# A two-layer hybrid block on one core: S5's backward rows in reverse order of time, and recurrent gates by 64-feature blocks, issued in steps

## The chip, the core and the metric

The kernel runs on one core of one Trainium2 chip. The metric is the device time of one execution in microseconds. An engine's name stands for its hardware: PE is TensorE, DVE VectorE, ACT ScalarE, POOL GpSimd, SP SyncE, whose queue issues the DMAs.

## The reference

Two layers act on 1024 latent and 256 context tokens of 1024 features. Cut to what matters here, a layer is

```python
h = _rmsnorm(x, norm_g[l]) * (1.0 + scale[:, None]) + shift[:, None]
ckv, krope, u_s5, x_lru, cq, x_pool, gpath, mlogit = jnp.split(h @ w_in[l], IN_SPLITS, axis=-1)
...
r = jax.nn.sigmoid(_block_diag(x, w_a, b_a).astype(f32))      # RG-LRU, both directions
i = jax.nn.sigmoid(_block_diag(x, w_x, b_x).astype(f32))      # 4 blocks of 64 x 64
log_a = -LRU_C * r * jax.nn.softplus(-lam.astype(f32))
b = jnp.sqrt(-jnp.expm1(2.0 * log_a)) * (i * x.astype(f32))
...
hc_re, hc_im = _s5_states(ucg, zero, zero, disc, rev)         # S5, dr = 0 and 1
hl_re, hl_im = _s5_states(ug, hc_re[:, last], hc_im[:, last], disc, rev)
y = y + _s5_readout(hl_re, hl_im, c_re[dr], c_im[dr])
...
y = y + jax.nn.sigmoid(ml[n]) * ((branches[n] * jax.nn.silu(gp[n])) @ w_branch[n])
```

Four branches read one projection `h @ w_in` of 6304 columns: latent attention (MLA), a diagonal state-space model of 16 groups with 64 states in either direction of time (S5), a gated linear recurrence in both directions (RG-LRU), and pooling. Each branch is multiplied by its gate path and projected, the four are summed under merge gates, `y @ w_out` follows, and the residual. The second layer needs no context output.

## The kernel before

**Tiles and products.** Features lie on partitions, tokens along the free side in three chunks `CH`: 256 context tokens and twice 512 latent ones. h, the normalised input of the layer, stays in SBUF as two float32r parts, high and low. A projection tile of 128 features and one chunk (`hgemm`, L181) is eight K-tiles of three float32r passes each (`gemm`, L174: low weight on high h, high on low, high on high), summed in a PSUM bank `pg`. `load_w` (L158) brings 128 x 512 weights by SyncE into a raw tile `wr` (two buffers); ScalarE copies the high part `wh`, VectorE subtracts for the low part `wl`. For the small weights of the branches these are `wph` and `wpl`. PSUM holds two banks `pg`, three `pS`, two `pm` and one `pP`. All matmuls go through the helper at L135, all ScalarE activations through L132, two-operand VectorE work through L117 and L120, and DMAs through L111, so operations are told apart by the tiles' names.

**The order.** The tile scheduler puts instructions in order by priority, which follows the text of the program except where a `with self.hp()` block lifts it. A tile that reuses memory waits for the last reader of what was there. Pools open by phase: `pr` and `pa` for the first part of a layer, `p5` with `pt` (attention) and then `pc` (merge) inside it, `pd` for the output projection. A layer (L1124) runs in this order: latent projections and keys (`mla_in`, `mla_kv`), the S5 input (`s5_in`), the recurrence's input and convolution (`lru_in`), `lru`, the query latents (`cq_in`), queries (`mla_q`), the pooling input (`pool_in`), pooling between gate tiles, attention, the other gate tiles, merge logits of the pooling branch, the merge, and the output projection.

**RG-LRU** (`lru`, L584). The weights of all gates, `wg`, come in one load as 128 x 128 matrices with two 64 x 64 blocks on the diagonal and zeros beside them. For each half f of the features, direction d and chunk, two float32 products with the tile `xl` give both gates, in a bank `pm` and a bank `pS`; one Tanh each takes 128 partitions out of it, to `l1` and `l2`. After the three chunks come Exp, Tanh, Square and Sqrt on ScalarE, products and scans over all tokens on VectorE, and after both directions a DMA of the branch output to DRAM.

**S5** (`s5`, L820) works on eight groups of two per layer. It is a Python generator: `logits` and `merge` step it between their tiles, and `lead` says how many steps lie between its parts. In a group the tokens are folded eight to a column: 160 columns, and `SC` = 192 with the 32 context columns once more behind the latent ones. The 128 partitions are 64 states forward and 64 backward. VectorE builds weights (`er`, `wb`, `wc`, `wk`) and phases (`ph`, from `hun`), both by way of `tm`; TensorE forms the inputs in `pS`, ScalarE copies them to `rqx`, VectorE rotates them by `ph`, scans them with a real decay, forward rows from column 0 up and backward rows from column 191 down, and rotates back into `er`; TensorE reads `er` with `wc` into `pS` (`pS<-er,wc`).

**Merge** (`merge`, L1020) goes over pooling, RG-LRU, MLA and S5 in that order. For each branch it multiplies output and gate (two loads `og`, then `b`), and for each of eight feature tiles j it makes the merge logits (not for pooling, whose logits were made before), the branch product `pm<-b,wph` / `wpl`, and the sum into `y`. `out_proj` (L1089) reads `ox`, the old x, by DMA, and forms the new one. Both `og` and `ox` are tiles of one tag in the standing pool `stream`, two buffers.

Of the kernel before, what the change touches and what calls it, by code (L numbers as in the profile page):

```python
# [42 lines left out]
V_D, V_CW, V_CB, V_LAM, V_BA, V_BX, V_PB, V_PS = 39, 41, 49, 51, 55, 59, 63, 65  # L43
NV = 67
# [19 lines left out]
class Net:  # L64
# [93 lines left out]
    def load_w(self, src, nk, small=False):  # L158
# [3 lines left out]
        with self.hp():  # L162
            for i in range(0, nk * m, 512):
# [3 lines left out]
                hi = self.whl.tile([128, w], F32R, tag=th, name=self.name(th), **kw)  # L167
                lo = self.whl.tile([128, w], F32R, tag=tl, name=self.name(tl), **kw)
# [19 lines left out]
    def prologue(self):  # L188
# [20 lines left out]
        self.ones, self.halfpi, self.halves, self.sgn = k[:, 0:1], k[:, 1:2], k[:, 2:4], k[:, 4:5]  # L209
# [220 lines left out]
    def cq_in(self, l, m, lat, pa):  # L430
# [153 lines left out]
    def lru(self, l, xls, oD, outs, pa, pr):  # L584
        nc, I, vec = self.nc, self.I, self.vec[l]
# [3 lines left out]
        hba = sp[:, 24:32]  # L589
# [15 lines left out]
        self.ts(hba, vec[:, V_BA:V_BA + 8], 0.5, None, ALU.mult, None)  # L605
        wg = self.t(pa, "wg", 1024)
        self.dma(wg, I["w_lru"][l])
        wgv = view(wg, 2, 2, 2, 128)
        for f in range(2):
            xl = xls[f]  # L610
            y = self.t(pr, "ly", NT)
            for d in range(2):
                c = 2 * d + f
                col = lambda a: a[:, c:c + 1]
                tr, ti, a, th = (self.t(pr, n_, w_)[:, 0:NT] for n_, w_ in (("l1", 1312), ("l2", 1312), ("l3", 8 * SC), ("l4", 8 * SC)))
                for s0, n in CH:
                    for g, dst in ((0, tr), (1, ti)):
                        ps = (self.pS() if g else self.ps())[:, 0:n]
                        self.mm(ps, wgv[:, d, g, f], xl[:, s0:s0 + n])
                        self.act(dst[:, s0:s0 + n], ps, AF.Tanh, bias=hba[:, 4 * g + c:4 * g + c + 1], scale=0.5)  # L620
# [16 lines left out]
            o0 = CH[outs[0]][0]  # L637
            self.dma(oD[f][:, o0:], y[:, o0:])


    def pool_in(self, l, lat, pa):
# [91 lines left out]
    def s5_head(self, l, p5):  # L733
# [86 lines left out]
    def s5(self, l, uF, uD, oD, lat, p5, lead):  # L820

# [15 lines left out]
        for q in range(16 // G):  # L837
# [595 lines left out]
```

## Time and profile before

| | |
|---|---|
| median of 3 runs | 2319.51 us (2313.85, 2319.51, 2320.29) |
| the profiled execution | 2318.8 us |
| its span on the core | 2317.0 us |
| mean granted TensorE clock | 0.996 |
| busy: TensorE, VectorE, ScalarE, GpSimd | 2265.9, 1545.9, 963.1, 208.7 us |
| mean busy share of the 16 DMA engines | 32.2% by the hardware queue |

The span is the time from the first to the last instruction of the profiled execution; its own time is 1.8 us longer. A busy time is the union of an engine's instructions. Matmuls are pipelined and overlap, so a record's duration is longer than what the pass costs; what it costs is the distance from its start to the next one's start. A granted clock of 1.00 is 2.4 GHz, a clock of 0.5 is 1.2 GHz, and a mean between them says that both were granted in the stretch. "Idle before" is the idle time of an engine just before a group of instructions, with what ended it.

### The profile page before, as it was taken

Reading aid. Unit: us, or ns where it says so; the run is one execution under the profiler, and the core shown is the slowest. Engines: PE = TensorE matmul, PEld = TensorE weight load, DVE = VectorE, ACT = ScalarE, POOL = GpSimd, SP = SyncE. Lnnn points to the kernel's source line nnn. Section 1 sums busy time; section 2 is a strip of 40 time slices with the busy share of each in tenths; the row PEclk is TensorE's granted clock in tenths of the full one; section 3 lists DMA queues with packets and bytes.
Section 4 is the critical chain, followed back from the end, with each engine's and each line's share of the span. In section 5 each row is a group of like instructions: output and inputs, shape, how many; then the busy total and the mean of one; then the engine's idle time right before and its main releaser. Section 6 shows DMA issues by size and latency. Waiting matters only on the chain.

```text
span 2317.0 us, 33029 instructions
## 1 busy us (share of the span) xinstructions
PE 2265.9 (98%) x11680; PEld 1847.4 (80%) x11680; DVE 1545.9 (67%) x3528; ACT 963.1 (42%) x1954; POOL 208.7 (9%) x261
## 2 busy tenths in 40 slices
PE   8999999999999999999999999999999899999999
PEld 3787878888788888788888787788888788877887
DVE  5665669776877888656455746688667878863253
ACT  4546656665312222312143436756664232322131
POOL 0000000000001121111122100000000011211100
PEclk9999999999999999999999999999999999999999
DMA  8150332211533223423334331332214331232134
GB/s 279 59 162 35 112 118 69 72 57 54 175 97 120 74 77 107 131 90 106 98 100 155 122 122 65 112 117 72 72 55 127 109 108 50 85 112 86 46 117 156
DMA packets 215750, 236.34 MB, mean 102 GB/s; under 512 B 78112, under 2 KB 141344, under 8 KB 215584
## 3 DMA queue, kind: packets, MB, share of 16 engines
q1 hardware_dynamic: 215072, 234.19, 32.2%
q8 instruction: 92, 1.51, 0.3%
q0 software_dynamic: 512, 0.03, 0.1%
q14 instruction: 74, 0.61, 0.1%
HBM read 175.70 MB, written 58.46 MB: 101 GB/s over the span
## 4 chain that ended last, share of the span: by engine, by line
PE 49%; DVE 5%; DMA 2%; ACT 1%; issue 1%; POOL 0%; SPq 0%; ACTq 0%; DVEq 0%; POOLq 0%
PE pg L135 34%; PE pS L135 6%; PE pm L135 5%; PE pP L135 3%; PE pm L138 1%; DVE wl L117 1%; DVE tm L117 1%; DVE st L120 1%; DMA wr<-in_w_out 1%; DMA s5g<-y 1%; DMA wr<-in_w_in 0%; DVE h L120 0%; PE pS L138 0%; ACT pt L132 0%; DVE er L117 0%
## 5 line engine op out<-in xcount | busy, mean ns | idle before, releaser
L135 PE MATMUL pg<-h,wh 128*128 128x512 f32 (+1 forms) x4608 | 1346.2, 374 | 0.2 <-DVE h L117 0.2
L135 PEld LDWEIGHTS pg<-h,wh 128*128 128x128 f32 x4608 | 829.0, 189 | 153.7 <-issue 4.5
L135 PE MATMUL pg<-h,wl 128*128 128x512 f32 (+1 forms) x2304 | 871.1, 378 | 1.8 <-DVE wl L117 1.6
L135 PEld LDWEIGHTS pg<-h,wl 128*128 128x128 f32 x2304 | 434.4, 189 | 80.5 <-issue 3.6
L117 DVE TENSOR_TENSOR wl<-wr,wh 128x512 fp32r<-128x512 f32 x268 | 190.5, 713 | 167.0 <-ACT wh L132 165.7
L132 ACT ACTIVATE wh<-wr 128x512 fp32r<-128x512 f32 x268 | 167.9, 628 | 272.9 <-PE pg L135 148.3
L132 ACT ACTIVATE st<-pg 128x512 f32<-128x512 f32 (+1 forms) x200 | 110.4, 552 | 350.9 <-PE pg L135 339.7
L117 POOL TENSOR_TENSOR y<-y,st 128x512 f32<-128x512 f32 (+1 forms) x120 | 153.6, 1280 | 733.8 <-DVE st L120 703.6
L135 PE MATMUL pm<-b,wph 128*128 128x512 f32 (+1 forms) x640 | 184.6, 373 | 1.6 <-DVE b L117 1.6
L132 ACT ACTIVATE P<-pS,sm,qs 128x512 f32<-128x512 f32 (+1 forms) x200 | 138.6, 702 | 45.3 <-DVE sm L124 43.2
L120 DVE SCALAR_TENSOR_TENSOR st<-st,pm 128x512 f32<-128x512 f32 (+1 forms) x120 | 75.6, 630 | 105.8 <-PE pm L135 105.3
L135 PE MATMUL pS<-k,q 128*128 128x512 f32 (+1 forms) x600 | 145.2, 365 | 0.5 <-DVE q L117 0.3
L135 PEld LDWEIGHTS pm<-b,wph 128*128 128x128 f32 x640 | 115.9, 189 | 24.4 <-DVE b L117 3.1
L135 PE MATMUL pP<-pt,v 128*128 128x256 f32 x656 | 126.9, 301 | 3.5 <-DVE pt L117 1.3
L135 PEld LDWEIGHTS pP<-pt,v 128*128 128x128 f32 x656 | 99.0, 188 | 35.6 <-ACT pt L132 21.9
L135 PE MATMUL pm<-b,wpl 128*128 128x256 f32 (+1 forms) x320 | 120.1, 376 | 5.0 <-ACT b L132 2.8
L117 DVE TENSOR_TENSOR pt<-pm,pt 128x512 fp32r<-128x512 f32 x164 | 106.9, 683 | 26.2 <-ACT pt L132 25.4
L518 DVE TENSOR_REDUCE sm<-pS 128x1 f32<-128x512 f32 (+1 forms) x200 | 113.3, 586 | 15.0 <-PE pS L135 13.1
L132 ACT ACTIVATE pt<-pm 128x512 fp32r<-128x512 f32 x164 | 91.0, 599 | 70.6 <-PE pm L138 70.1
L135 PEld LDWEIGHTS pS<-k,q 128*128 128x128 f32 x600 | 98.8, 189 | 18.0 <-ACT P L132 4.5
L138 PE MATMUL pm<-ident,P 128*128 128x128 f32 x656 | 106.3, 274 | 0.2 <-ACT P L132 0.2
L120 DVE SCALAR_TENSOR_TENSOR pP<-wa,cv,pP 128x256 f32<-128x256 f32 x196 | 95.3, 486 | 14.1 <-DMA wa<-in_w_ada 10.4
(244 smaller groups left out, 2500.2 us busy)
## 6 DMA issues: line engine op xcount, KB each, us to landing
wr<-in_w_in SPq DMA_DIRECT2D x196, 256.0 KB, 2.7
wa<-in_w_ada SPq DMA_DIRECT2D x96, 256.0 KB, 2.9
wr<-in_w_out SPq DMA_DIRECT2D x64, 256.0 KB, 2.9
gD<-st SPq DMA_DIRECT2D x32, 256.0 KB, 2.0
tD<-st SPq DMA_DIRECT2D x32, 256.0 KB, 2.2
og<-oD SPq DMA_DIRECT2D x32, 256.0 KB, 2.7
og<-gD SPq DMA_DIRECT2D x32, 256.0 KB, 2.9
wr<-in_w_branch SPq DMA_DIRECT2D x64, 128.0 KB, 2.0
```

The costliest lines, as they stand in the source:

```text
L117: (eng or self.nc.vector).tensor_tensor(out=out, in0=a, in1=b, op=op)
L120: self.nc.vector.scalar_tensor_tensor(out=out, in0=a, scalar=s, in1=b, op0=op0, op1=op1)
L132: self.nc.scalar.activation(out=out, in_=a, func=func, scale=scale, **kw)
L135: self.nc.tensor.matmul(out=out, lhsT=lhsT, rhs=rhs, start=start, stop=stop)
L138: self.nc.tensor.transpose(out=out, in_=in_, identity=ident)
L518: nc.vector.tensor_reduce(out=mx3[:, i:i + 1], in_=S, axis=AX.X, op=ALU.max)
```

## The change

**S5.** The backward rows are copied out of PSUM in reverse order of time, from columns 32 to 191, so that both directions run over 160 columns from the first to the last; the copy to `rqx` becomes two, of 64 partitions each. Phases, rotation and scan have 160 columns a group in place of 192, the two scans of 64 partitions become one of 128, and the read-back turns the backward rows round again.

**The recurrence's gates.** `xb` holds two stacked versions of `xl`, one per block b of 64 features: its own 64 rows carry the high float32r part, the other 64 the low part. The weights come per direction and half, 128 x 256, by the raw tiles `wr`, stacked to fit: `wgh` is the high part of the block's two gate matrices in both halves of the rows, `wgl` the low part on the block's own rows and zero on the others (GpSimd's memset). A gate tile is then two accumulated float32r passes for each block, `wgl` and `wgh`, and comes out of PSUM in two Tanh of 64 partitions, one per gate.

**The steps.** `lru` becomes a generator that stops after the first latent chunk of each (f, d) and after each (f, d). `cq_in` and `pool_in` step it after each latent chunk, eight times in all, and `pool_in` moves ahead of `mla_q`. The output DMA goes out after d = 1 of each half.

**Pools.** `og` and `ox` move from `stream` to `pc` and `pd`, `wph` and `wpl` from the standing weight pool to `pc`.

```diff
-                hi = self.whl.tile([128, w], F32R, tag=th, name=self.name(th), **kw)
-                lo = self.whl.tile([128, w], F32R, tag=tl, name=self.name(tl), **kw)
+                pool = small or self.whl
+                hi = pool.tile([128, w], F32R, tag=th, name=self.name(th), **kw)
+                lo = pool.tile([128, w], F32R, tag=tl, name=self.name(tl), **kw)
...
-    def cq_in(self, l, m, lat, pa):
+    def cq_in(self, l, m, lat, pa, bg):
...
+                if ci > 0:
+                    next(bg)
...
+            xb = view(self.t(pa, "xb", 2 * NT, dt=F32R), 2, NT)
+            for s0, n in CH:
+                for b in range(2):
+                    src, hi = xl[H[b], s0:s0 + n], xb[H[b], b, s0:s0 + n]
+                    self.act(hi, src, AF.Copy)
+                    self.tt(xb[H[1 - b], b, s0:s0 + n], src, hi.bitcast(F32), ALU.subtract)
...
+                raw = self.wraw.tile([128, 512], F32, tag="wr", name=self.name("wr"))[:, 0:256]
+                wh, wl = (view(self.t(pa, n_, 256, 2, F32R), 2, 128) for n_ in ("wgh", "wgl"))
+                with self.hp():
+                    self.dma(raw, I["w_lru"][l][:, 256 * c:256 * c + 256])
+                    raw = view(raw, 2, 128)
+                    self.act(wh, raw, AF.Copy)
+                    for b in range(2):
+                        nc.gpsimd.memset(wl[H[1 - b], b].bitcast(F32), 0.0)
+                        self.tt(wl[H[b], b], raw[H[b], b], wh[H[b], b].bitcast(F32), ALU.subtract)
                 for s0, n in CH:
-                    for g, dst in ((0, tr), (1, ti)):
-                        ps = (self.pS() if g else self.ps())[:, 0:n]
-                        self.mm(ps, wgv[:, d, g, f], xl[:, s0:s0 + n])
-                        self.act(dst[:, s0:s0 + n], ps, AF.Tanh, bias=hba[:, 4 * g + c:4 * g + c + 1], scale=0.5)
+                    cols = slice(s0, s0 + n)
+                    for b in range(2):
+                        o = H[b]
+                        ps = (self.pS() if b else self.ps())[:, 0:n]
+                        self.mm(ps, wl[:, b], xb[:, b, cols], True, False)
+                        self.mm(ps, wh[:, b], xb[:, b, cols], False, True)
+                        self.act(tr[o, cols], ps[o], AF.Tanh, bias=hba[o, c:c + 1], scale=0.5)
+                        e = 4 + 2 * c + b
+                        self.act(ti[o, cols], ps[H[1 - b]], AF.Tanh, bias=hba[H[1 - b], e:e + 1], scale=0.5)
+                    if s0 == CH[1][0]:
+                        yield
...
-            o0 = CH[outs[0]][0]
-            self.dma(oD[f][:, o0:], y[:, o0:])
...
+                    o0 = CH[outs[0]][0]
+                    self.dma(oD[f][:, o0:], y[:, o0:])
+                yield
...
+            ph = view(self.t(p5, "ph", 2 * n), 2, G, 160)
             dr, di = ph[:, 0], ph[:, 1]
-            P4 = [128, G, 12, 16]
+            P4 = [128, G, 10, 16]
             wide = lambda x: x.rearrange("p g (m j) -> p g m j", j=16)
...
             for gg in range(G):
                 ps = view(self.pS(), 2, SC)
                 for k in range(2):
                     self.mm(ps[:, k], wbv[:, gg, k], u[:, gg])
-                self.act(xv[:, :, gg], ps, AF.Copy)
-            m1, m2 = view(tm, 2, G, SC)[:, 0], view(tm, 2, G, SC)[:, 1]
-            rt = self.t(p5, "er", 2 * n)
-            rv = view(rt, 2, G, SC)
+                self.act(xv[F_, :, gg], ps[F_, :, 0:160], AF.Copy)
+                self.act(xv[B_, :, gg], ps[B_, :, 32:SC][:, :, ::-1], AF.Copy)
...
             for k in range(2):
                 for gg in range(G):
-                    decay = bc(hd["rho"][:, G * q + gg:G * q + gg + 1], [128, SC])
-                    a, b = rv[:, k, gg], xv[:, k, gg]
-                    v.tensor_tensor_scan(out=b[F_], data0=decay[F_], data1=a[F_], initial=0.0, op0=ALU.mult, op1=ALU.add)
-                    v.tensor_tensor_scan(out=b[B_][:, ::-1], data0=decay[B_], data1=a[B_][:, ::-1], initial=0.0,
-                                         op0=ALU.mult, op1=ALU.add)
+                    decay = bc(hd["rho"][:, G * q + gg:G * q + gg + 1], [128, 160])
+                    v.tensor_tensor_scan(out=xv[:, k, gg], data0=decay, data1=rv[:, k, gg], initial=0.0, op0=ALU.mult, op1=ALU.add)
...
-                self.tt(rv[B_, k, :, 32:160], m1[B_, :, 33:161], m2[B_, :, 33:161], op)
+                self.tt(rv[B_, k, :, 32:160], m1[B_, :, 31:159][:, :, ::-1], m2[B_, :, 31:159][:, :, ::-1], op)
...
-                        o, gt = (self.stream.tile([128, 512], F32, tag="og", name=self.name("og"), bufs=2)[:, 0:n] for _ in range(2))
+                        o, gt = (pc.tile([128, 512], F32, tag="og", name=self.name("og"), bufs=2)[:, 0:n] for _ in range(2))
...
-                wp = self.load_w(I["w_branch"][l, b, j], 2, True)
+                wp = self.load_w(I["w_branch"][l, b, j], 2, pc)
...
-                        x0 = self.stream.tile([128, 512], F32, tag="og", name=self.name("ox"), bufs=2)[:, 0:n]
+                        x0 = pd.tile([128, 512], F32, tag="og", name=self.name("ox"), bufs=2)[:, 0:n]
...
             xl = self.lru_in(l, pa, pads)
-            self.lru(l, xl, oD[LRUB], lat, pa, pr)
-            self.cq_in(l, m, lat, pa)
+            rec = self.lru(l, xl, oD[LRUB], lat, pa, pr)
+            self.cq_in(l, m, lat, pa, rec)
+            xp = self.pool_in(l, lat, pa, rec)
             self.mla_q(l, m, lat, pa)
-            xp = self.pool_in(l, lat, pa)
...
         out["w_lru"].append(np.concatenate(
-            [_blockdiag(a[n][l, d, 2 * f:2 * f + 2]) for d in range(2) for n in ("lru_w_a", "lru_w_x") for f in range(2)], 1))
+            [np.tile(np.concatenate([a[n][l, d, 2 * f + b] for n in ("lru_w_a", "lru_w_x")[::1 - 2 * b]], 1), (2, 1))
+             for d in range(2) for f in range(2) for b in range(2)], 1))
```

Instructions by name and count, before and after. PE: the 48 float32 gate products (32 of 512 columns, 16 of 256, two records each) become 64 float32r passes of 512 and 32 of 256. ACT: 48 Tanh of 128 partitions become 96 of 64, 32 copies to `rqx` of 128 partitions become 64 of 64, and there are 24 copies to `xb`, 8 to `wgh`, and 25 table loads for 23. DVE: 128 S5 scans of 64 x 192 become 64 of 128 x 160, S5's operations on 384 columns have 320, and 24 subtractions for `xb` and 16 for `wgl` are new. POOL: 16 memsets more. SP: two loads of 128 x 1024 become eight of 128 x 256.

**TensorE, layer 0, the recurrence's gates.** Ahead of them stands the end of the projection that gives `xl`. Before, in the order of instructions:

```order
L135 MATMUL pg_1526<-h_84,wl_1496 128x512
L135 MATMUL pg_1526<-h_84,wh_1495 128x512 x2
L135 MATMUL pm_1598<-xl_1479,wg_1591 128x256
L135 MATMUL pS_1601<-xl_1479,wg_1591 128x256
L135 MATMUL pm_1604<-xl_1479,wg_1591 128x512
L135 MATMUL pS_1607<-xl_1479,wg_1591 128x512
L135 MATMUL pm_1610<-xl_1479,wg_1591 128x512
L135 MATMUL pS_1613<-xl_1479,wg_1591 128x512
```

After the change:

```order
L135 MATMUL pg_1602<-h_84,wl_1570 128x512
L135 MATMUL pg_1602<-h_84,wh_1569 128x512 x2
L135 MATMUL pm_1687<-xb_1660,wgl_1680 128x256
L135 MATMUL pm_1687<-xb_1660,wgh_1679 128x256
L135 MATMUL pS_1692<-xb_1660,wgl_1680 128x256
L135 MATMUL pS_1692<-xb_1660,wgh_1679 128x256
L135 MATMUL pm_1697<-xb_1660,wgl_1680 128x512
L135 MATMUL pm_1697<-xb_1660,wgh_1679 128x512
L135 MATMUL pS_1702<-xb_1660,wgl_1680 128x512
L135 MATMUL pS_1702<-xb_1660,wgh_1679 128x512
L135 MATMUL pg_1707<-h_84,wl_1564 128x512
L135 MATMUL pg_1707<-h_84,wh_1563 128x512 x2
```

The gate products stood one behind the other, 24 in a row in a layer; now the first chunks of a (f, d) are followed by projection tiles of the query latents. Between the first gate and the first product of attention TensorE has 359 projection passes of 512 columns in place of 320 in layer 0, and 420 in place of 330 in layer 1; behind the last product of attention in layer 1 it has 1630 in place of 1740.

**VectorE, layer 1, S5's third group.** These rows build its weights from the powers `hao` and the matrices `cm`. Before:

```order
L117 TENSOR_TENSOR tm_17557<-hao_16900,cm_17539 128x256 x2
L854 MEMSET er_17551 128x128
L117 TENSOR_TENSOR er_17551<-tm_17557 128x256
L117 TENSOR_TENSOR tm_17557<-hao_16900,cm_17539 128x256 x2
L117 TENSOR_TENSOR er_17551<-tm_17557 128x256
L117 TENSOR_TENSOR tm_17557<-hao_16900,cm_17539 128x256 x2
L117 TENSOR_TENSOR wc_17559<-tm_17557 128x2x8x16
L117 TENSOR_TENSOR tm_17557<-hao_16900,cm_17539 128x256 x2
L117 TENSOR_TENSOR wc_17559<-tm_17557 128x2x8x16
L117 TENSOR_TENSOR tm_17557<-hun_16912 128x384 x2
```

After:

```order
L117 TENSOR_TENSOR tm_17751<-hao_17098,cm_17733 128x256
L120 SCALAR_TENSOR_TENSOR og_18285<-og_18285,og_18286 128x512
L120 SCALAR_TENSOR_TENSOR y_18065<-y_18065,pm_18131 128x512
L117 TENSOR_TENSOR er_17745<-tm_17751 128x256
L120 SCALAR_TENSOR_TENSOR y_18065<-y_18065,pm_18139 128x512
L117 TENSOR_TENSOR wpl_18173<-wr_18171,wph_18172 128x256
L117 TENSOR_TENSOR tm_17751<-hao_17098,cm_17733 128x256 x2
L120 SCALAR_TENSOR_TENSOR y_18066<-y_18066,pm_18154 128x512
L117 TENSOR_TENSOR er_17745<-tm_17751 128x256
L117 TENSOR_TENSOR tm_17751<-hao_17098,cm_17733 128x256
L120 SCALAR_TENSOR_TENSOR y_18066<-y_18066,pm_18162 128x512
L117 TENSOR_TENSOR wpl_18196<-wr_18194,wph_18195 128x256
```

Rows of the pooling branch (`y<-y,pm`), of `og` and of `wpl` now stand between the rows of S5: 16 rows `y<-y,pm` and seven more of `wpl` ahead of the third group's scans. From attention's last product up to the third group's first `pS<-er,wc` TensorE now has 120 projection and 99 branch passes in place of 188 and none; from there to the fourth group's, 70 projection and 21 branch passes in place of 112 and 120.

**SyncE, layer 0, the first loads of `ox`.** The loads are issued in this order. Before, in the merge:

```order
L111 DMA wr_10295<-in_w_in 128x512
L111 DMA og_10123<-gD_697 128x512
L111 DMA wr_10301<-in_w_branch 128x256
L111 DMA wa_10335<-in_w_ada 128x2x256
L111 DMA ox_11434<-in_xT 128x512
L111 DMA wa_10350<-in_w_ada 128x2x256
L111 DMA ox_11463<-in_xT 128x256
L111 DMA wa_10383<-in_w_ada 128x2x256
L111 DMA wa_10398<-in_w_ada 128x2x256
```

After, at the start of the output projection:

```order
L111 DMA wa_11409<-in_w_ada 128x2x256
L111 DMA wr_11512<-in_w_out 128x512
L111 DMA wr_11518<-in_w_out 128x512
L111 DMA wr_11582<-in_w_out 128x512
L111 DMA wr_11588<-in_w_out 128x512
L111 DMA wr_11656<-in_w_out 128x512
L111 DMA wr_11662<-in_w_out 128x512
L111 DMA ox_11524<-in_xT 128x512
L111 DMA ox_11553<-in_xT 128x256
L111 DMA ox_11594<-in_xT 128x512
L111 DMA wr_11730<-in_w_out 128x512
```

Before, the first two loads of `ox` went out among the loads of the merge (`wr<-in_w_branch`, and `wa`, weights of the next modulation); after, six loads of output weights stand ahead of the first `ox`, which reuses the memory of the merge tile `y0`.

## Rows read from the trace of the kernel before

**Rows 1.** The page, parts 1 and 2: busy per engine; PE's share in 40 slices

```profile
PE 2265.9 (98%) x11680; PEld 1847.4 (80%) x11680; DVE 1545.9 (67%) x3528; ACT 963.1 (42%) x1954; POOL 208.7 (9%) x261
...
PE   8999999999999999999999999999999899999999
```

**Rows 2.** TensorE's waits, whole span: total us, times, longest us

```profile
PE pS L135 <- DVE er L117: 10.6, 6, 2.6
```

**Rows 3.** Timeline of TensorE, 165 to 178 us: start us, us, what, records

```profile
166.21 0.59 PE L135 MATMUL pS<-xl,wg 128*128 128x256 f32 x2
166.64 1.02 PE L135 MATMUL pm<-xl,wg 128*128 128x512 f32 x2
167.50 1.02 PE L135 MATMUL pS<-xl,wg 128*128 128x512 f32 x2
...
174.22 0.28 PE L135 MATMUL pg<-h,wl 128*128 128x256 f32 x1
...
174.58 0.28 PE L135 MATMUL pg<-h,wl 128*128 128x256 f32 x1
...
177.06 0.40 PE L135 MATMUL pg<-h,wl 128*128 128x512 f32 x1
177.29 0.63 PE L135 MATMUL pg<-h,wh 128*128 128x512 f32 x2
177.76 0.40 PE L135 MATMUL pg<-h,wl 128*128 128x512 f32 x1
```

**Rows 4.** Windows: length, PE, PEld, DVE, ACT, POOL busy us, PEclk, DMA share, GB/s

```profile
165.00:235.00 70.00, 67.82 (x319) 51.50 (x318) 39.02 (x41) 47.34 (x63) 0.37 (x6) 1.00 0.19 64
1403.00:1464.00 61.00, 60.70 (x242) 43.73 (x241) 36.59 (x34) 45.80 (x59) 0.37 (x6) 1.00 0.15 50
1767.20:1831.80 64.60, 56.83 (x262) 45.80 (x260) 58.94 (x136) 19.48 (x44) 1.51 (x2) 0.95 0.55 168
700.00:920.00 220.00, 215.47 (x1154) 183.44 (x1153) 184.66 (x397) 56.69 (x125) 40.83 (x35) 0.99 0.31 93
```

**Rows 5.** Groups by form, VectorE: count, busy us, mean ns, idle us before

```profile
L117 DVE TENSOR_TENSOR tm<-rqx,ph 128x384 f32<-128x384 f32 x128 | 73.4, 602 | 17.5 <-ACT rqx L132 16.2
L117 DVE TENSOR_TENSOR tm<-hao,cm 128x256 f32<-128x256 f32 x128 | 52.5, 443 | 1.6
L936 DVE TENSOR_TENSOR_SCAN rqx<-hkeep,er 64x192 f32<-64x192 f32 x64 | 36.5, 570 | 1.3
...
L120 DVE SCALAR_TENSOR_TENSOR y<-y,pm 128x512 f32<-128x512 f32 x32 | 21.8, 682 | 5.8 <-PE pm L135 5.5
...
L634 DVE TENSOR_TENSOR_SCAN l<-l,l,l 128x1024 f32<-128x1024 f32 x4 | 9.4, 2348 | 0.1
...
L632 DVE TENSOR_TENSOR_SCAN l<-l,l 128x256 f32<-128x256 f32 x4 | 2.7, 684 | 0.0
```

**Rows 6.** Groups by form, ScalarE

```profile
L132 ACT ACT_TABLE_LOAD x23 | 29.5, 1283 | 1.2 <-PEq L1425 0.7
...
L132 ACT ACTIVATE rqx<-pS 128x384 f32<-128x384 f32 x32 | 15.6, 498 | 9.3 <-PE pS L135 9.3
...
L132 ACT ACTIVATE l<-pm,lsp 128x512 f32<-128x512 f32 x16 | 11.0, 688 | 2.5 <-PE pm L135 2.4
...
L132 ACT ACTIVATE l<-pm,lsp 128x256 f32<-128x256 f32 x8 | 3.8, 472 | 1.2 <-DVE qtmp L124 1.1
```

**Rows 7.** TensorE's waits, 1750 to 1900 us

```profile
PE pS L135 <- DVE er L117: 7.1, 3, 2.6
```

**Rows 8.** Timeline of TensorE, 1774 to 1782 us, its last entry the wait

```profile
1778.78 1.22 PE L135 MATMUL pS<-er,wc 128*128 128x128 f32 x4 [2.21 <-DVE er L117]
```

**Rows 9.** Timelines of SyncE's queue and VectorE, 1179 to 1184 us; tile ox

```profile
1179.60 0.90 SPq L111 DMA_DIRECT2D wr<-in_w_out  x2
...
1183.15 0.75 DVE L120 SCALAR_TENSOR_TENSOR x<-pg,mod,ox 128x512 f32<-128x512 f32 x1 [0.40 <-PE pg L135]
...
DMA to landing us min/median/max: 2.0/2.6/6.8
```

More of the change, by code (lines that the diff above doesn't have):

```diff
@@ L42 @@
 V_BADA, V_G, V_QN, V_KVN, V_QG, V_KG, V_KRG = 0, 24, 32, 34, 35, 37, 38
-V_D, V_CW, V_CB, V_LAM, V_BA, V_BX, V_PB, V_PS = 39, 41, 49, 51, 55, 59, 63, 65
-NV = 67
+V_D, V_CW, V_CB, V_LAM, V_BA, V_BX, V_PB, V_PS = 39, 41, 49, 51, 55, 59, 67, 69
+NV = 71
 def view(ap, *dims):
@@ L156, in gain_split, with load_w @@
         self.stt(lo, src, gain, hi.bitcast(F32), ALU.mult, ALU.subtract)
-    def load_w(self, src, nk, small=False):
+    def load_w(self, src, nk, small=None):
         m = src.shape[1] // nk
@@ L208, in prologue @@
         ms(k[32:64, 6:7], 0.0)
-        self.ones, self.halfpi, self.halves, self.sgn = k[:, 0:1], k[:, 1:2], k[:, 2:4], k[:, 4:5]
+        self.ones, self.halfpi, self.halves = k[:, 0:1], k[:, 1:2], k[:, 2:4]
         self.qmask = [k[:, 5:6], k[:, 6:7]]
@@ L588, in lru @@
         e, z, z2, acc, p4, m4 = (sp[:, 4 * i:4 * i + 4] for i in range(6))
-        hba = sp[:, 24:32]
+        hba = sp[:, 24:36]
         self.stt(e, lam, -1.0, lam, ALU.mult, ALU.max)
@@ L604, in lru @@
         self.ts(m4, acc, -4.0, None, ALU.mult, None)
[L605 to L608, printed above, removed]
+        self.ts(hba, vec[:, V_BA:V_BA + 12], 0.5, None, ALU.mult, None)
+        H = (slice(0, 64), slice(64, 128))
         for f in range(2):
             xl = xls[f]
+            xb = view(self.t(pa, "xb", 2 * NT, dt=F32R), 2, NT)
[4 more added lines that the diff above has]
+                    self.tt(xb[H[1 - b], b, s0:s0 + n], src, hi.bitcast(F32), ALU.subtract)
             y = self.t(pr, "ly", NT)
@@ L636, in lru, with pool_in @@
                     self.tt(y, y, tr, ALU.add)
[L637 to L641 removed]
+                    o0 = CH[outs[0]][0]
+                    self.dma(oD[f][:, o0:], y[:, o0:])
+                yield
+    def pool_in(self, l, lat, pa, bg):
         out = []
@@ L654, in pool_in @@
                     self.act(xp[:, off:off + n], ps, AF.Copy)
+                if ci > 0:
+                    next(bg)
             out.append(xp)
@@ L800, in s5_head @@
         self.tt(rho, t2, t2, ALU.mult)
-        un = view(self.t(p5, "hun", 928), 2, 16, 29)
+        un = view(self.t(p5, "hun", 864), 2, 16, 27)
         a_r, a_i = cs, sn
@@ L805, in s5_head @@
             a_r, a_i = o_r, o_i
-        self.ts(a_i, a_i, self.sgn, None, ALU.mult, None)
-        for (w_r, w_i), last in (((un[:, 0, :, 0:17], un[:, 1, :, 0:17]), 16), ((un[:, 0, :, 17:29], un[:, 1, :, 17:29]), 11)):
+        self.ts(a_i, a_i, -1.0, None, ALU.mult, None)
+        for (w_r, w_i), last in (((un[:, 0, :, 0:17], un[:, 1, :, 0:17]), 16), ((un[:, 0, :, 17:27], un[:, 1, :, 17:27]), 9)):
             v.memset(w_r[:, :, 0:1], 1.0)
@@ L912, in s5 @@
                 yield
-            xt = self.t(p5, "rqx", 1024)[:, 0:2 * n]
-            xv = view(xt, 2, G, SC)
+            xv = view(self.t(p5, "rqx", 1024), 2, G, 160)
             wbv, wkv = view(wb, G, 2, 128), view(wk, G, 128)
@@ L1393, in _layout @@
              np.concatenate([_fv(a["lru_conv_w"][l][k]) for k in range(4)], 1), _fv(a["lru_conv_b"][l]),
-             two(a["lru_lambda"][l]), two(a["lru_b_a"][l]), two(a["lru_b_x"][l]),
+             two(a["lru_lambda"][l]), two(a["lru_b_a"][l]), np.tile(a["lru_b_x"][l].reshape(8, 64).T, (2, 1)),
              _fv(a["pool_b"][l]), _fv(a["pool_scale"][l])], 1))
```

11 lines of the change are left out of this document (5 added, 6 removed).

## The prediction

> **What bounds the kernel now.** The page comes first. Its engine shares say that TensorE is busy for 2265.9 us, 98% of the span, and the 40 slices show it at 9 from the second slice to the last but for one 8; VectorE follows with 1545.9 us, so no other engine can be the limit over the whole span [rows 1]. The list of TensorE's waits comes second: of what other engines make it wait for after the start, the S5 branch's tile er from VectorE is the largest, 10.6 us [rows 2]. So nearly every microsecond of TensorE work taken away should leave the span, and few places have waits to give back. What a pass costs I take from the timeline, from its start to the next one's, because the durations of pipelined matmuls overlap: three float32r passes of 512 columns take 0.70 us (177.06 to 177.76), three of 256 columns 0.36 (174.22 to 174.58), but one full float32 product of 512 columns, two records, takes 0.86 us (166.64 to 167.50) and one of 256 columns 0.43 (166.21 to 166.64) [rows 3]. The windows by stretch come last: where the recurrent gates run, ScalarE is busy 47.3 of 70 us in layer 0 and 45.8 of 61 us in layer 1; where S5 opens in layer 1, VectorE is busy 58.9 of 64.6 us and TensorE's granted clock averages 0.95 [rows 4].
>
> **The gates on TensorE.** Before, each layer has 24 float32 products, 16 of 512 columns and 8 of 256: 16 x 0.86 + 8 x 0.43 = 17.2 us, 34.4 us in both. After, the same tiles come from two accumulated float32r passes for each of two 64-feature blocks: 64 passes of 512 columns and 32 of 256 in the two layers, 64 x 0.234 + 32 x 0.118 = 18.8 us [rows 3]. Removed: **15.6 us**, all on the engine that sets the end.
>
> **The gates on ScalarE and VectorE.** Each gate tile now leaves PSUM in two activations of 64 partitions. Columns set the time, so I price the 48 extra ones as the old ones: 32 x 0.688 + 16 x 0.472 = 29.6 us. At the same prices the 24 copies to xb are 14.8 us and the eight copies of weights 3.8 us; two more table loads are 2.6 us. Together 50.8 us, 25.4 us a layer [rows 6]. VectorE gains 24 low parts, at most 0.682 each, and 16 differences of 128 columns, at most 0.443 each, 23 us in the two layers [rows 5]; it was busy 39.0 of 70 us there [rows 4], which covers it. GpSimd's 16 memsets have an idle engine. SyncE's queue gets eight loads of 128 KB in place of two of 512 KB, in the raw buffers that also carry the projections' weights, each issued a step ahead.
>
> ScalarE is the tight one. The 25.4 us go into idle time of 22.7 us in layer 0 and 15.2 us in layer 1 [rows 4], while the order has TensorE run 39 and 90 more projection passes of 512 columns than before between the first gate and the first attention product, which fills. If the added time stays inside idle time nothing is lost, and the 2.2 and 0.3 us that TensorE idled there could go too; if it spills over wholly, (25.4 - 22.7) + (25.4 - 15.2) = 13 us come back. I take **+3 us**, nearer to the good end, since TensorE's idle time in these rows is so small beside a ScalarE busy for 70% and other products stand between the gates; I keep -2 and +13. About the table loads the row says 1.28 us each, 23 of them [rows 6]. The Trainium skill, "ScalarE: Activation LUTs", section "What ACT_TABLE_LOAD costs", has a rule that speaks against steps which alternate functions: a switch of sets costs a drain of about 1.38 us beside the load, 2.66 us in all. By it the added time would be 53.6 us and the bad end 16 us; no row of this trace shows such a drain, and the sum goes by the row.
>
> **S5 on VectorE.** Turning the backward rows round lets both directions use 160 columns in place of 192 and one scan in place of two. An operation of 384 columns takes 0.602 us and one of 256 takes 0.443, so one of 320 about 0.52: 16 of them a group (eight on rqx, four on hun, two into er, two into ph) save 1.3 us. Eight scans at 0.57 become four; from 0.684 for 256 columns and 2.348 for 1024 a scan of 160 is an estimated 0.476, so 4.5 us become 1.9 [rows 5]. That is 3.9 us a group, 62 us in 16 groups. ScalarE pays two copies of 320 elements, each at most the 0.498 of the one of 384 that they replace [rows 6]: up to 16 us, where it is busy a quarter of the time [rows 4].
>
> What this is worth is read from where TensorE waits. Of the 10.6 us for er, 7.1 lie in layer 1's opening and so 3.5 in layer 0 [rows 2, 7]. In layer 0 VectorE was busy 184.7 of 220 us in the merge [rows 4]; with 31 us less it loses its queue, and I take **-3**. In layer 1 the opening is VectorE's: TensorE idled 2.21 us until er came at 1778.78 [rows 8]. Three groups save 11.7 us there, but the order in the document shows what takes their place: 16 rows y<-y,pm of the pooling branch, 0.682 us each [rows 5], 10.9 us, and seven more wpl now stand ahead of the third group's scans. So the third er is not earlier. TensorE's cover changes too. Behind the last attention product the order has 1630 projection passes of 512 columns in place of 1740: 110 x 0.234 = 25.7 us were moved ahead of attention's end, into the stretch of the gates. Up to the third er it has 120 projection and 99 branch passes in place of 188 projection passes, 31 more, 7 us; but ahead of the fourth group stand 70 and 21 in place of 112 and 120. I take **-2** here; the bounds are -12 (all 7.1 us, the clock's 0.05 x 64.6 = 3.2, and a little in later groups) and +26 (the moved work missing in full).
>
> **Pools.** og and ox leave the standing pool. In the merge og now lies beyond attention's last tile and has nothing to wait for. At layer 0's output projection the first two ox were loaded during the merge; now they stand behind six weight loads and wait for a tile of the merge, y0. Before, the fifth and sixth of these loads were issued from 1179.60 to 1180.50 and the first x<-pg,mod,ox began at 1183.15; an ox takes 2.6 us to land, at most 6.8 [rows 9]. 1180.5 + 2.6 = 1183.1 is just in time, 1187.3 is 4 us late, with a second PSUM bank before TensorE notices: **+0.5**. Layer 1's ox take tiles that S5 has long left.
>
> **Sum.** -15.6 + 3 - 3 - 2 + 0.5 = -17 us against the profiled execution's 2318.8 us: **2302 us**. The median of the three runs, 2319.51, lies 0.7 above that execution, so the change is -0.75%; a measurement of this kernel can tell about 0.3%, 7 us, from no change.
>
> **Rivals.** *S5's waits go in full.* If VectorE no longer ends the waits, -12 in layer 1 and -4 in layer 0 replace -2 and -3: 2291 us. For it: 62 of 1546 us less on VectorE. Against it: the rows put into the gap. 0.15. *ScalarE becomes the bound in the gates' stretch.* Tanh pieces come late, PSUM banks stay full, TensorE waits: +13 in place of +3 and little from S5: 2315 us. For it: 25.4 us into 15.2. Against it: the products between the gates. 0.15. *The fill is missing where S5 opens in layer 1, and the kernel gets slower.* If VectorE's chain through the first four groups sets the time alone, the 25.7 us spent early come back as waits: 2302 + 26 = 2328 us. It decides from some 24 us of new waits on. For it: 58.9 of 64.6 us. Against it: the 99 branch passes moved in. 0.04. The rows put the clock there at 0.95. The Trainium skill, "TensorE: Matmul & The Clock Gate", section "HAM oscillation — how this bites in real kernels", says that work after such idling starts at the lower of the two clocks; by that rule 2328 would be this rival's floor, and the trace agrees in direction with its 0.95. *The passes are not cheaper.* Each has new weights; were one as long as half a float32 product, 0.43 us, nothing would be saved: 2318 us. The long products change weights at each pass too, at 0.234, so 0.04.
>
> **Numbers.** The forecast has 0.62. Faster than 2312.5 are nearly all of it, the first rival and half of the second: 0.83. Within 0.3%, to 2326.5, lies the rest of these: 0.13. Slower: 0.04. The range, 2289 to 2315 us, leaves out the last two rivals and the tails of the first two.
>
> **What would show it.** Right: wgh and wgl passes follow each other at 0.23 us, TensorE's busy time falls by about 16 us, VectorE's by 40 or more, ScalarE's rises by 50 to 65, and waits for er in layer 1 stay near 7 us. Wrong: new TensorE waits for ScalarE's tile l between 140 and 230 us; waits for er beyond 20 us with the clock well below 0.95 in S5's opening; or a wait for ox at layer 0's output projection.

## The result and the profile after

The change makes the kernel faster by half a per cent: median 2309.59 us against 2321.52 before, ratio 0.995 (95% interval 0.9938 to 0.9962), so 12 us where 17 were forecast. One of the ten executions of the change took 7476 us, for a reason that no profile shows; the ratio goes without it and the median hardly moves with it. Measured once more beside a control (the kernel before as a kernel of its own), the change has 2312.50 and 0.9943 (0.9927 to 0.996).

The profiled execution of the change took 2315.7 us, 6 us over its median, and the one shown of before 2.7 us under its own; read against each other they show only 3 us. So where lost time is compared, below, both come from a later series, in which the kernel before (span 2323.3 us) and the change (2307.9) ran on one chip. The page of the first profile, parts 1 and 2, against [rows 1]:

```profile
PE 2261.1 (98%) x11680; PEld 1845.7 (80%) x11680; DVE 1503.2 (65%) x3502; ACT 1027.9 (44%) x2068; POOL 210.8 (9%) x277
...
PE   8999999999999999999999999999999999999999
```

TensorE is busy as much as ever, VectorE for 42.7 us less, ScalarE for 64.8 us more. TensorE's waits over the whole span, against [rows 2]:

```profile
PE pS L135 <- DVE er L117: 5.8, 7, 2.0
PE pS L135 <- ACT wk L132: 3.8, 2, 3.0
```

The waits for er are nearly halved (5.0 us of them still lie in layer 1's opening); those for wk, a copy of S5 on ScalarE, come to 3.8 us where the same list of before had 0.7. The timeline of TensorE at a gate of layer 1, against [rows 3]:

```profile
1422.32 0.28 PE L135 MATMUL pm<-xb,wgl 128*128 128x256 f32 x1
1422.44 0.27 PE L135 MATMUL pm<-xb,wgh 128*128 128x256 f32 x1
...
1422.78 0.40 PE L135 MATMUL pm<-xb,wgl 128*128 128x512 f32 x1
1423.02 0.39 PE L135 MATMUL pm<-xb,wgh 128*128 128x512 f32 x1
1423.24 0.39 PE L135 MATMUL pS<-xb,wgl 128*128 128x512 f32 x1
```

Passes of 512 columns follow each other at 0.23 us, those of 256 at 0.12. The groups by form of VectorE, then of ScalarE, against [rows 5, 6]:

```profile
L117 DVE TENSOR_TENSOR tm<-rqx,ph 128x320 f32<-128x320 f32 x128 | 62.2, 519 | 11.4 <-ACT rqx L132 10.7
L961 DVE TENSOR_TENSOR_SCAN rqx<-hkeep,er 128x160 f32<-128x160 f32 x64 | 27.5, 474 | 0.0
L117 DVE TENSOR_TENSOR xb<-xl,xb 64x512 fp32r<-64x512 f32 x16 | 11.0, 686 | 0.5
```

```profile
L132 ACT ACT_TABLE_LOAD x25 | 32.1, 1283 | 3.9 <-DVE ly L117 2.4 <-PEq L1450 0.7 <-DVE er L124 0.3
L132 ACT ACTIVATE rqx<-pS 64x320 f32<-64x320 f32 x64 | 27.6, 432 | 10.0 <-PE pS L135 9.3
L132 ACT ACTIVATE l<-pm,lsp 64x512 f32<-64x512 f32 x32 | 21.9, 684 | 0.5
L132 ACT ACTIVATE l<-pS,lsp 64x512 f32<-64x512 f32 x32 | 21.9, 683 | 0.7
L132 ACT ACTIVATE xb<-xl 64x512 fp32r<-64x512 f32 x16 | 10.1, 629 | 6.6 <-DVE xl L120 6.3
```

A Tanh of 64 partitions takes 0.684 us, one of 128 took 0.688: splitting a tile by partitions doubles the time.

**How lost time is counted.** Every matmul record has its undisturbed distance to the next one's start (0.234 and 0.118 us for float32r passes, 0.43 and 0.215 for each of the two records of a float32 product, 0.11 to 0.16 for the small ones of S5 and of the sums). Their sum over a stretch is TensorE's work; the stretch's length less its work is lost, to waits and to a lower clock. Over the whole program the work is 2220.2 us before and 2204.6 after, 15.6 less, and on the one chip 98.6 us are lost before and 99.2 after. Three stretches matter: from the first gate to the first product of attention ("gates", both layers together), and from attention's last product to the last `er,wc` of S5 ("S5", each layer). All come from one profile of each kernel. Two profiles of one kernel differ here by up to 0.6 us in the gates and 2.1 us in a column of S5, and a profile can stand off its kernel's median (S5's reversal alone: 5.1 us under it), so small differences between rows say nothing:

| kernel | ratio to before | gates lost | S5, layer 0, lost | S5, layer 1, work | lost |
|---|---|---|---|---|---|
| before (control) | 1.000 | 6.0 | 16.8 | 267.8 | 15.6 |
| the change, again | 0.9943 | 17.5 | 10.9 | 242.0 | 12.4 |
| S5's reversal alone | 0.9975 | 5.9 | 11.5 | 269.7 | 5.1 |
| pools alone | 0.9974 | 5.9 | 16.3 | 267.8 | 11.4 |
| float32 gates in steps, S5, pools | 0.9933 | 4.5 | 10.9 | 264.7 | 7.7 |
| change without S5's reversal | 1.0035 | 17.0 | 21.0 | 244.4 | 23.0 |
| change without steps | 1.0021 | 38.0 | 15.0 | 256.5 | 4.5 |
| without steps and reversal | 1.0157 | 41.4 | 23.9 | 253.3 | 20.2 |
| change, xb on VectorE | 0.9921 | 17.8 | 9.3 | 245.3 | 9.0 |
| change, xb on GpSimd | 0.9911 | 15.6 | 15.4 | 245.3 | 7.1 |
| the same, Squares on GpSimd | 0.9949 | 21.7 | 11.2 | 249.5 | 9.8 |

The windows of the four stretches (gates of layers 0 and 1, S5 of layers 0 and 1), with the columns of [rows 4], first of the kernel before, then of the change, in the later series:

```profile
165.00:311.20 146.20, 143.48 (x722) 113.81 (x720) 86.28 (x138) 89.06 (x129) 0.38 (x6) 1.00 0.31 98
1407.90:1526.90 119.00, 118.58 (x516) 89.88 (x514) 76.74 (x111) 80.54 (x109) 0.38 (x6) 1.00 0.31 102
570.70:919.50 348.80, 338.35 (x1793) 287.20 (x1792) 284.14 (x643) 90.03 (x202) 43.09 (x38) 0.99 0.37 107
1771.60:2054.90 283.30, 273.52 (x1260) 223.33 (x1259) 236.11 (x475) 79.84 (x177) 37.73 (x30) 0.98 0.35 98
```

```profile
173.40:326.00 152.60, 147.68 (x760) 119.32 (x758) 90.01 (x149) 109.72 (x162) 1.18 (x10) 1.00 0.29 94
1403.30:1541.90 138.60, 135.15 (x606) 104.32 (x604) 84.61 (x127) 106.00 (x151) 1.18 (x10) 1.00 0.31 99
584.90:912.80 327.90, 322.12 (x1717) 273.21 (x1716) 252.23 (x613) 93.45 (x211) 42.02 (x38) 0.99 0.39 112
1785.80:2040.20 254.40, 245.90 (x1151) 201.57 (x1150) 202.49 (x444) 83.72 (x186) 37.67 (x30) 0.99 0.38 105
```

In the gates TensorE's idle time (length less busy) goes from 2.7 and 0.4 us to 4.9 and 3.5, with ScalarE at 109.7 of 152.6 us. In layer 1's S5 both the length and VectorE's busy time fall, and the gap between length and TensorE's busy time stays, 9.8 and 8.5.

### The profile page after: what moved, and what is told of

Read it like the earlier page. It is cut to its first block, busy times and chain, and to the rows that moved or that the text cites. A ratio compares the mean times of both kernels' runs of the same rounds, so it can differ in the third digit from the quotient of the medians.

```text
span 2313.9 us, 33181 instructions
## 1 busy us (share of the span) xinstructions
PE 2261.1 (98%) x11680; PEld 1845.7 (80%) x11680; DVE 1503.2 (65%) x3502; ACT 1027.9 (44%) x2068; POOL 210.8 (9%) x277
## 4 chain that ended last, share of the span: by engine, by line
PE 47%; DVE 6%; ACT 3%; DMA 2%; issue 1%; POOL 0%; SPq 0%; DVEq 0%; ACTq 0%; POOLq 0%
PE pg L135 32%; PE pS L135 5%; PE pm L135 5%; PE pP L135 3%; ACT l L132 1%; PE pm L138 1%; DVE tm L117 1%; DVE wl L117 1%; DVE st L120 1%; DMA wr<-in_w_in 1%; DMA og<-gD 0%; DVE er L117 0%; PE pS L138 0%; ACT wh L132 0%; ACT pt L132 0%
## 5 line engine op out<-in xcount | busy, mean ns | idle before, releaser
L117 DVE TENSOR_TENSOR wl<-wr,wh 128x512 fp32r<-128x512 f32 x268 | 196.8, 736 | 194.0 <-ACT wh L132 188.0
L519 DVE TENSOR_REDUCE sm<-pS 128x1 f32<-128x512 f32 (+1 forms) x200 | 113.4, 587 | 29.2 <-PE pS L135 28.3
L135 PEld LDWEIGHTS pP<-pt,v 128*128 128x128 f32 x656 | 99.2, 188 | 37.0 <-ACT pt L132 24.2
```

The lines of the kernel that those rows point to most:

```text
L117: (eng or self.nc.vector).tensor_tensor(out=out, in0=a, in1=b, op=op)
L135: self.nc.tensor.matmul(out=out, lhsT=lhsT, rhs=rhs, start=start, stop=stop)
L519: nc.vector.tensor_reduce(out=mx3[:, i:i + 1], in_=S, axis=AX.X, op=ALU.max)
```

## The experiments

**S5 alone.** Only S5's hunks, on the kernel before:

```diff
-    v.tensor_tensor_scan(out=b[F_], data0=decay[F_], data1=a[F_], ...)
-    v.tensor_tensor_scan(out=b[B_][:, ::-1], data0=decay[B_], ...)
+    v.tensor_tensor_scan(out=xv[:, k, gg], data0=decay, data1=rv[:, k, gg], ...)
```

> The kernel before with the reversal of S5's backward rows alone: 160 columns, one scan, two copies out of PSUM; gates, steps and pools as before. Theory A (TensorE's passes carry the gain, S5 gives only the waits for er): 2 to 6 us less than before, a ratio of 0.998, with VectorE's busy time down by 45 to 60 us and TensorE's modelled work unchanged. Rival B (S5's relief of VectorE carries the gain of 12 us and the gates give back what they save): 9 to 14 us less, a ratio of about 0.995.

2317.94 us, ratio 0.9975 (0.996 to 0.999). That is 7.3 us less than before, between theory A's 2 to 6 and rival B's 9 to 14 and nearer to A. Theory A's mechanism is there: of the waits for er in layer 1's opening, 7.1 us before [rows 7], 0.5 are left. VectorE is busy 1483.9 us, 62.0 less than [rows 1], as the prediction had it.

**The change without S5's reversal.** S5's hunks taken back, all else stays.

> The changed kernel with S5 as before: gates in two float32r passes, steps and pools stay. Theory A: 6 to 10 us less than before, a ratio of 0.996 to 0.997, so 2 to 6 us more than the whole change. Rival B: within 3 us of before. Rival C (the two parts need each other, since the filler spent early comes back as waits where S5 opens in layer 1): slower than before, waits for er there above 12 us.

2330.69 us, 1.0035 (1.0022 to 1.0048): slower than before. Theories A and B fall, C holds in its sign, though not in its marker: in layer 1's S5 the waits for er come to 5.4 us, those for b, a tile of the merge, to 5.7 and those for wk to 2.5. TensorE has 244.4 us of work in that stretch where it had 267.8, and loses 23.0 where it lost 15.6. The gates take the larger part: they lose 17.0 us where the control lost 6.0.

**The change without steps.** `lru` runs in one piece, and `pool_in` goes back behind `mla_q`.

```diff
-            rec = self.lru(l, xl, oD[LRUB], lat, pa, pr)
+            for _ in self.lru(l, xl, oD[LRUB], lat, pa, pr):
+                pass
+            rec = iter(range(99))
```

> The changed kernel with the recurrence issued in one piece, as before, and the pooling input behind the queries; the gates keep their two float32r passes, S5 and the pools stay changed. TensorE's work is the same as in the change. Theory A (the steps keep ScalarE's longer work off TensorE's path): 5 to 15 us slower than the change, with TensorE waiting for ScalarE's tile l in the gates' stretch, 4 us or more in a layer. Rival D (the scheduler's priorities spread the gates anyway and the steps give nothing): within 3 us of the change.

2328.84 us, 1.0021 (1.0007 to 1.0034), 0.8% or 18 us more than the change beside its control. Theory A, and a little more: the gates lose 38.0 us in place of 17.5, and TensorE's idle time in front of l comes to 4.4 us in either layer. Layer 0's part of it:

```profile
PE pm L135 <- ACT l L132: 2.9, 4, 1.2
PE pS L135 <- ACT l L132: 1.5, 4, 0.9
```

The timelines of ScalarE and of TensorE where its gates begin in layer 0:

```profile
170.32 1.38 ACT L132 ACTIVATE l<-pS,lsp 64x512 f32<-64x512 f32 x2
171.72 1.38 ACT L132 ACTIVATE l<-pm,lsp 64x512 f32<-64x512 f32 x2
173.13 1.39 ACT L132 ACTIVATE l<-pS,lsp 64x512 f32<-64x512 f32 x2
```

```profile
170.35 0.39 PE L135 MATMUL pm<-xb,wgl 128*128 128x256 f32 x1 [1.18 <-ACT l L132]
...
171.75 0.50 PE L135 MATMUL pS<-xb,wgl 128*128 128x512 f32 x1 [0.90 <-ACT l L132]
172.09 0.40 PE L135 MATMUL pS<-xb,wgh 128*128 128x512 f32 x1
173.16 0.79 PE L135 MATMUL pm<-xb,wgl 128*128 128x512 f32 x1 [0.68 <-ACT l L132]
```

ScalarE has no gap and takes 1.4 us to empty a bank (two Tanh); TensorE fills one in two passes, 0.47 us, and waits. Before, a bank took TensorE 0.86 us and ScalarE 0.69 [rows 3, 6]: ScalarE waited for TensorE. The cheaper product, with its second Tanh, turned this round where the gates stand in a row. With the steps this wait nearly goes. TensorE's waits in the gates of layer 0 in the whole change (173 to 326 us):

```profile
PE pP L135 <- DVE sc L117: 1.4, 2, 0.9
PE pS L135 <- DVE xb L117: 1.3, 2, 1.1
...
PE pm L135 <- DVE xb L117: 0.6, 1, 0.6
PE pS L135 <- ACT l L132: 0.3, 1, 0.3
```

Here most of the idle time is put down to VectorE: xb, whose low part it subtracts, and sc, a product from the pooling input that stands among the gates now.

**Without steps and without the reversal.** Both edits together.

> The gates' two float32r passes and the pools alone: no steps, S5 as before. Theory A, with the parts adding up: the time of the run without steps plus what S5 gives, 2 to 6 us. If S5 gives its share only with the steps (the stretch where S5 opens has less filler with them), this run lies within 2 us of the one without steps alone.

2359.24 us, 1.0157 (1.0143 to 1.0171). Neither expectation holds: S5's reversal is worth 30 us here, 7 by itself and some 20 beside the steps. The parts do not add up. What waits cost is seen with the clock; windows of 2 us at the gates of layer 0 of this kernel:

```profile
168.00:170.00 2.00, 1.45 (x6) 1.00 (x6) 1.93 (x3) 1.94 (x5) 0.40 (x2) 1.00 0.00 0
170.00:172.00 2.00, 0.80 (x2) 0.50 (x2) 1.95 (x4) 1.94 (x4) 0.00 (x0) 0.71 0.00 0
...
176.00:178.00 2.00, 0.50 (x2) 0.00 (x1) 1.44 (x2) 1.22 (x2) 0.00 (x0) 0.50 0.00 0
178.00:180.00 2.00, 2.00 (x9) 2.00 (x10) 0.00 (x0) 0.00 (x0) 0.00 (x0) 0.50 0.38 100
180.00:182.00 2.00, 2.00 (x10) 1.79 (x9) 0.49 (x1) 0.63 (x1) 0.00 (x0) 0.73 0.43 130
182.00:184.00 2.00, 2.00 (x11) 1.64 (x11) 0.20 (x1) 0.00 (x0) 0.00 (x0) 1.00 0.32 97
```

TensorE is busy for 1.45 and 0.80 us of the first two windows, idle in front of xb and l, and in the second the granted clock falls; from there until about 181 us TensorE works at half the clock, 1.2 GHz. A further wait, 1.5 us from 176 to 178, comes at the low clock already. The granted clock averages 0.984 over this span and 0.994 over the control's; (1 - clock) times the span is 38 and 14 us, so up to 24 of the 34 us by which this run is slower can be clock. It is a bound, as TensorE is idle for a part of the time at the low clock. The Trainium skill, "TensorE: Matmul & The Clock Gate", section "HAM oscillation — how this bites in real kernels", has the same course for a kernel whose products wait for DMAs: the work behind such a wait starts at the lower clock. This trace agrees in the course, with 0.50 in full windows, behind shorter waits, for ScalarE and VectorE.

**Pools alone, and again beside the control.** The moves of og, ox, wph and wpl, on the kernel before.

> The kernel before with the pools alone changed: og and ox in the merge's and the output projection's pool, wph and wpl in the merge's. Nothing else. If the pools carry nothing: a ratio within 0.9985 to 1.0015 of before, up to 1 us of new waits for ox where layer 0's output projection begins. If they carry part of the gain: 0.997 or less.

> The kernel before, unchanged, as a kernel of its own in the place that S5's reversal alone and the pools alone had: a control. If such a comparison has no bias: a ratio within 0.999 to 1.001. If it gives a few us to whatever stands there, it lies at 0.997 as those two did, and their gains are not to be believed.

> The pools alone once more, beside the control. If the 7 us of the first measurement are real: 0.996 to 0.9985 again and at least 3 us below the control. If not: within 2 us of the control.

The pools alone have 2319.45 us, 0.9972 (0.9959 to 0.9984), and 2318.68, 0.9974 (0.996 to 0.9989). The control has 1.000 (0.9988 to 1.0012), so the 6 to 7 us are real; I had counted +0.5. Of the 7.0 us between the two spans of the later series, 4.2 lie in layer 1's S5 and 1.8 in layer 0's merge behind S5. In layer 1's opening the lists of who waited for og, 1765 to 1860 us, are, in the control

```profile
  ACT b L132: 8.1, 2
  DVE og L120: 0.6, 1
```

and with the pools changed

```profile
  ACT b L132: 2.2, 2
  DVE b L117: 0.8, 2
```

ScalarE, which also owes S5 its copies, stood 8.1 us before a copy of b and now 2.2. That this makes the 4 us is not shown, nor what ox, wph and wpl do. The reverse, the change without the pools, was not tried: xb takes 10 KB of each partition, and the pools free 8 for it.

**Float32 gates in steps.** The change, but with the products, Tanh and weights of before in the gates.

```diff
+                        self.mm(ps, wgv[:, d, g, f], xl[:, s0:s0 + n])
+                        self.act(dst[:, s0:s0 + n], ps, AF.Tanh, bias=hba[:, 4 * g + c:4 * g + c + 1], scale=0.5)
+                    if s0 == CH[1][0]:
+                        yield
```

> The changed kernel with the gates' float32 products of before (128 partitions to a Tanh, one load of weights, no xb), issued in steps; S5 and the pools stay changed. TensorE has 15.6 us more work than in the change, ScalarE some 25 us a layer less. If the steps only keep ScalarE's added work off TensorE's path: the time of S5's reversal alone, a ratio of 0.996 to 0.9985, and under 8 us lost by TensorE in the two gate stretches. If the steps are worth something by themselves: 0.995 or less, as good as the change without its cheaper passes.

2309.88 us, 0.9933 (0.9919 to 0.9947): with 15.6 us more of TensorE work as fast as the change. Under 8 us are lost in the gates, as in the first case of the expectation; the time is that of the second, which counts nothing for the pools. S5 and the pools alone make 0.9975 x 0.9973 = 0.9948, an estimate, since the two were not run together. By it the steps add some 0.15%, within the intervals. Its windows of the two gate stretches:

```profile
173.90:310.80 136.90, 135.14 (x673) 106.42 (x671) 79.48 (x128) 86.64 (x125) 0.18 (x3) 1.00 0.27 88
1406.20:1520.10 113.90, 113.90 (x497) 86.64 (x496) 72.03 (x109) 79.22 (x109) 0.37 (x6) 1.00 0.30 94
```

In layer 1 TensorE has no idle time at all; the stretches lose 4.5 us in place of 17.5.

**The whole change, again.**

> The whole change once more, to stand beside the runs with float32 gates and with xb on GpSimd (0.9933 and 0.9911 to before). If the cheaper passes are given back in full: 0.994 to 0.996, not better than float32 gates in steps. If they carry the gain as forecast: 0.992 or less.

2312.50 us, 0.9943 (0.9927 to 0.996), not better than float32 gates in steps: given back in full.

**xb's high parts on VectorE, and on GpSimd.**

```diff
-                    self.act(hi, src, AF.Copy)
+                    nc.gpsimd.tensor_copy(out=hi, in_=src)
```

> The whole change, but xb's 24 high parts are copied by VectorE, 7 us a layer less on ScalarE. If ScalarE is what makes TensorE lose 18 us in the two gate stretches (6.5 before): 3 to 8 us less than the change, a ratio of 0.992 to 0.994 to before. If it is the chain over VectorE (it is named as often in the waits there, for xb and sc): the change's 0.995, or up to 4 us worse.

> The whole change, but xb's 24 high parts are copied by GpSimd, which has nothing else to do there; ScalarE has 7 us a layer less and VectorE no more. If ScalarE is the limit of the gate stretches: 3 to 8 us less than the change, 0.992 to 0.994. If the length of the chain from xl over the high to the low part counts, GpSimd's slower copies make it worse: 0.996 or more, with TensorE waiting for xb.

On VectorE 2307.13 us, 0.9921 (0.9906 to 0.9935); on GpSimd 2304.12 us, 0.9911 (0.9895 to 0.9926), the best of all and 0.3% under the change. The size is as expected on VectorE and a little more on GpSimd; the place is not: the gates still lose 17.8 and 15.6 us. With xb on GpSimd 5.3 us less are lost in layer 1's S5 and 4.5 more in layer 0's; the order leaves 3.3 and 5.4 us more work there. The profiles of the two kernels differ by 3.9 us in all, the ratios by some 7 us, so about half of the gain has no place. How the scheduler comes to this order stays open. Still, in the same series the cheaper passes with xb on GpSimd are 5.8 us faster than float32 gates in steps (2304.12 and 2309.88), where as made they are not.

**The Squares on GpSimd as well.**

```diff
-                self.act(tr, a, AF.Square)
+                self.tt(tr, a, a, ALU.mult, nc.gpsimd)
```

> The whole change with xb's high parts and the recurrence's eight Squares (1280 columns, 1.27 us each on ScalarE) on GpSimd: ScalarE has 5 us a layer less again. If ScalarE still makes TensorE lose the 15.6 us of the gate stretches with xb on GpSimd: 2 to 5 us less than that run, a ratio of 0.989 to 0.9905. If the waits there are now VectorE's (sc) or the chain of the recurrence: 0.991 to 0.993.

2313.32 us, 0.9949 (0.9933 to 0.9966), 9 us more than without it; neither case of the expectation holds. ScalarE's busy time falls by 9.9 us, but the gates lose 21.7. GpSimd's group:

```profile
L117 POOL TENSOR_TENSOR l<-l 128x1280 f32<-128x1280 f32 x8 | 18.8, 2345 | 115.2 <-ACT l L132 108.6 <-issue 6.6
```

It takes 2.35 us for what ScalarE did in 1.27, in the middle of each chain from Tanh to scan.

## Why the prediction was right, and where it was not

The time lies in the range and the sign is right, but the sum came out by two errors that cancel, which is luck. On the one chip TensorE's work gives -15.6 us and what it loses changes by +11.5 in the gates, -5.9 and -3.2 in S5, -3.6 in layer 0's merge behind S5 (8.6 to 5.0) and +2.0 in attention: -15 us, against -17. So the gates lost 8.5 us more than the +3, and S5, the pools and the rest together gave 6.2 us more than the -4.5 of the sum.

- **The gates on TensorE**, -15.6: right to the tenth, and so are the distances of 0.23 and 0.12 us. The marker was badly chosen: TensorE's busy time fell by 4.8 us in the first pair of profiles and 13.8 in the second, since records behind a wait last longer.
- **ScalarE's and VectorE's added work**: sizes right. The 96 Tanh take 58.8 us, 29.2 more than before (29.6 forecast), xb 13.4 (14.8), S5's copies 12.0 more (up to 16), ScalarE in all 64.8 more (50 to 65). VectorE's low parts and differences take 19.0 us (at most 23).
- **The step that failed** is the term for the gates' loss, "I take +3 us, nearer to the good end, since TensorE's idle time in these rows is so small". It was +11.5, close to the other end, 13. TensorE's idle time was small because its float32 products were slower than ScalarE's activations, bank by bank, and the change reverses that; a sum over the stretch (25.4 us into 22.7 and 15.2) does not show it, the times for one bank do. Where the gates stand in a row, this makes TensorE wait (38.0 us lost without the steps). That it also makes the 11.5 us with the steps is not shown: there the waits for l are 1.3 us in both layers, and none of them lies between 140 and 230 us, where the prediction looked for them; those for xb are 2.6, those for VectorE's sc 2.2. What is shown is that the new gates as a whole cost it, since float32 gates with the same steps lose 4.5 us in place of 17.5; how it divides between the second Tanh, the chain over xb and VectorE stays open. A spill-over of ScalarE's total, as the prediction's bad end has it, it is not: in layer 0's stretch ScalarE is idle for 42.9 of 152.6 us. Taking 7 us a layer off ScalarE gave back 1.9 us there with GpSimd, none with VectorE. What follows for the net: the cheaper passes earn nothing as made, since float32 gates in steps are as fast.
- **The table loads**: each still takes 1.283 us, and the trace does not bear out the drain that the prediction cites from the Trainium skill, "ScalarE: Activation LUTs", section "What ACT_TABLE_LOAD costs". In the first profile of the change:

```profile
1431.46 0.62 ACT L132 ACTIVATE wh<-wr 128x512 fp32r<-128x512 f32 x1
1432.10 1.28 ACT L132 ACT_TABLE_LOAD   x1
1433.39 0.47 ACT L132 ACTIVATE l<-pm,lsp 64x256 f32<-64x256 f32 x1
```

The load begins 0.02 us behind the copy, and the Tanh 0.01 us behind the load; over all 25 loads ScalarE's idle time in front of them is 3.9 us, where 25 drains of 1.38 would be 34.5. The sum rightly went by the row.

- **S5**, -3 and -2: -5.9 and -3.2, or -2.3 and -0.5 in the first pair. As the text had it, it is a balance: 25.8 us of work left layer 1's stretch (25.7 forecast), and the reversal pays for them. The rival in which the missing fill makes the kernel slower had 0.04. Its sign comes without the reversal (1.0035), at a smaller price than its 24 us: layer 1's S5 loses 7.4 us more than the control, and the gates' 11.0 do the rest. With the reversal this price was paid.
- **Pools**, +0.5: wrong. They give 6 to 7 us by themselves. I looked at ox, where no wait came; in layer 1's opening og, which I took for free, held up ScalarE for 8.1 us before and 2.2 after; what that is worth to TensorE is not shown.
- So of the 0.5% hardly anything is owed to the cheaper passes: with float32 products in their place the time is the same (0.9933), S5's reversal and the pools make it up by the product of their ratios, and the gates in their new form need the steps not to cost 18 us more.

## What to carry to other kernels

On a kernel bound by TensorE, a cheaper product in a row of products counts only if the engine that empties PSUM keeps up bank by bank: compare the two durations for one bank before and after, not the idle sums of the stretch alone. Work that fills a gap early is missing where the next gap is, so test the parts of a change apart and together; here one part is worth 7, 20 or 30 us, depending on the others. A move of buffers deserves a run of its own.

## What the runs showed of the hardware

GpSimd rounds 64 x 512 values to float32r in 0.74 us, near ScalarE's 0.63, but multiplies 128 x 1280 in 2.35, where ScalarE's Square takes 1.27. An activation on 64 partitions takes as long as one on 128 (0.684 and 0.688 us at 512 columns). A table load on ScalarE takes 1.28 us with no idle time beside it that would be a drain. And the clock can make up most of the slowest run's extra time: up to 24 of 34 us.
